# A decoder layer on one core: sums of gathered expert rows one step after their fetch, splits ordered behind them, residual work pinned to steps 32 to 46

## The chip, the core and the metric

The kernel runs on one core of a Trainium2 chip. The core has five engines that each work through a queue of their own in order: TensorE (PE, with its weight loads PEld), VectorE (DVE), ScalarE (ACT), GpSimd (POOL) and SyncE (SP, which here only issues transfers). Transfers run on 16 DMA engines. The metric is the device time of one execution in microseconds (us).

## The reference

One post-norm decoder layer on 256 tokens with 2048 channels. The part that the change touches is the last one, the sum over the chosen experts' output rows:

```python
u_sel = u[expert]
v_sel = v[expert]
act = jax.nn.gelu(jnp.einsum('td,thkd->thk', xc, u_sel).astype(jnp.float32), approximate=False)
return jnp.einsum('thk,thkd->td', (gate * act).astype(x.dtype), v_sel)
```

There are 16,384 experts, and every token takes 128 of them (8 heads of 16). Then `h = layer_norm(alpha * h + ffn)`.

## The kernel before

The kernel does not gather whole rows. For the first 1536 output channels it builds a dense matrix `S` of weights (expert by token, most of it zero) in SBUF and multiplies it on PE with the whole table `v_d`. For the last 512 channels it gathers the chosen rows of `v_g` by indirect DMA, one slot of 128 tokens at a time: 2 token tiles by 128 slots are 256 gathers of 256 KB, each followed by one multiply-add into `accg` on DVE (L813).

**The v stage.** It is the last long stage of the kernel. Its loop (L836) runs 124 steps `i2`. A step needs the weights of 128 experts (`weights`, L765: the part `step_of(i2)` of `S`, split in two) and three units of `v_d`, 128 x 512 each. I number the units through: unit m is unit m % 3 of step m // 3. Every float32 operand is split in a rounded part and a rest (`split`, L93): ACT casts `hi` (L94), DVE subtracts `lo` (L95). PE then does three products for each of the two token tiles (L119, L120, L121): six matmuls a unit, 18 a step. Four `hi`/`lo` pairs are in rotation, so splits run at most four units ahead of PE.

**Where the units lie.** A unit lands either in one of four `raw` buffers (`load_unit`, L100, on SP's queue) or in a part of `S` that is no longer needed (`v_unit`, L791). 23 units, all before step 13, use `raw`; all later ones use freed parts of `S`, which come free at the rate of half a part a step, so that loads run further and further ahead.

**Gathers.** `add_gathered` (L809) issues the gathers of a step on POOL (`v_gather`, L799) and writes each sum behind its gather. `spread` deals the 256 gathers out over steps 0 to 119. The rows land in three buffers `g`; from step `LEND` = 24 on, four of seven also use `raw`.

**Residual.** `residual` (L819) prepares alpha's operand for the last norm: 8 calls, written at even steps 32 to 46. Each loads two pieces of the first norm's scale and shift into the one buffer `g1` and two pieces of `z_dram` into `pre` (SP), and does four elementwise operations on POOL (L827, L828).

**The tail.** The last four steps are multiplied from `S` unsplit (L885), with weights copied into `last` (L854).

**What sets the order.** The program is written by a scheduler that sorts by priority and by its own estimate of times; `high_priority` draws the unit loads and splits ahead. `tc.issue_after(x)` adds one constraint: what is written in the block on the engine of x comes behind x in that engine's queue. What carries no such constraint may go far from where it is written.

Of the kernel before, what the change touches and what calls it, by code (L numbers as in the profile page):

```python
# [15 lines left out]
ALU = mybir.AluOpType  # L16
AX = mybir.AxisListType

P = 128
T = 256  # L20
NT = T // P
# [36 lines left out]
LEAD = 5  # L58
LAG = 1
KEEP0 = 40  # L60
LEND = 24
GL = 4
GVE = 120
ED = 2
EA = 2
TAIL_POOL = ((0, 1, 2), (0,))
# [5 lines left out]
def layer(ctx, tc, A, out):  # L72
    nc = tc.nc
# [14 lines left out]
        return psB.tile([P, 512], F32, name=name, tag="b")  # L88

    last_split, last_copy, last_load, last_moment = [None], [None], [None], [None]  # L90
    after_unit = [None]

    def split(hi, lo, src, eng=None):  # L93
        last_copy[0] = nc.scalar.copy(hi, src).ins  # L94
# [28 lines left out]
    e_idx = small.tile([P, NT, SLOTS], I32, name="e_idx")  # L123
# [3 lines left out]
    z_dram = dram.tile([NT, P, D], F32, name="z_dram")  # L127
# [368 lines left out]
    def step_of(i2, sl=slice(0, T)):  # L496
        return S[:, i2 // 2, sl.start // 2:sl.stop // 2, i2 % 2, :]
# [7 lines left out]
    def paired(a):  # L505
        return a.rearrange("p (t j) -> p t j", j=2)
# [156 lines left out]
    def spread(i, i0, i1):  # L663
        n = i1 - i0
        return gorder[len(gorder) * min(max(i - i0, 0), n) // n:len(gorder) * min(max(i - i0 + 1, 0), n) // n]
# [133 lines left out]
    def v_gather(i2, tt, slot):  # L799
        if i2 >= LEND and count[0] % (GB + RB) >= GB:  # L800
            g = raw_unit()
        else:
            g = gath.tile([P, GV], F32, name="g", bufs=GB)
        count[0] += 1
        nc.gpsimd.indirect_dma_start(out=g, out_offset=None, in_=A["v_g"],  # L805
                                     in_offset=bass.IndirectOffsetOnAxis(ap=e_idx[:, tt, slot:slot + 1], axis=0))
        return g

    def add_gathered(i2):  # L809
        with tc.issue_after(last_split[0]):  # L810
            for tt, slot in spread(i2, 0, GVE):
                g = v_gather(i2, tt, slot)
                nc.vector.scalar_tensor_tensor(accg[:, tt], g, pd[:, tt, slot:slot + 1], accg[:, tt],  # L813
                                               op0=ALU.mult, op1=ALU.add)


    pre = [[big.tile([P, 512], F32, name="pre", tag=f"{s}{q}") for q in (0, 3, 4, 5)] for s in "hl"]
# [1 line left out]
    def residual(c, hf):  # L819
        g1 = small.tile([P, 2, T], F32, name="g1", tag="h_gath")  # L820
        sl = slice(c * 512 + hf * T, c * 512 + (hf + 1) * T)
        for i in range(2):
            nc.sync.dma_start(g1[:, i], A["ln1"][i:i + 1, sl].broadcast_to([P, T]))
        for tt in range(NT):
            o = pre[tt][c][:, hf * T:(hf + 1) * T]
            nc.sync.dma_start(o, z_dram[tt][:, sl])
            nc.gpsimd.tensor_tensor(o, o, g1[:, 0], op=ALU.mult)  # L827
            nc.gpsimd.tensor_tensor(o, o, g1[:, 1], op=ALU.add)  # L828

    def finish(tt, c, lo, hi, src):  # L830
        o = pre[tt][c][:, lo:hi]
# [4 lines left out]
    for i2 in range(P - GL):  # L836
        wt = weights(i2, tokens if i2 == 0 else [slice(0, T)])
        units = []
        for c in range(NC):
            raw = v_unit(i2, c)  # L840
            units.append(load_unit(A["v_d"][i2 * NC + c], raw))
            if i2:
                for tt in range(NT):
                    product(wt, tt, c, units[c], i2)
        if i2 == 0:
            for tt in range(NT):
                for c in range(NC):
                    product(wt, tt, c, units[c], 0)
        add_gathered(i2)
        if 32 <= i2 < 48 and i2 % 2 == 0:  # L850
            residual((i2 - 32) // 4, (i2 - 32) // 2 % 2)
    last = [big.tile([P, 2, T], F32, name="last", tag="l2"), small.tile([P, 2, T], F32, name="last", tag="h_gath")]
    for j in range(GL):
        nc.scalar.copy(paired(last[j // 2][:, j % 2]), step_of(P - GL + j))  # L854
    for tt in range(NT):
        finish(tt, 3, 512 - GV, 512, accg[:, tt])
        nc.vector.bn_stats(stats[tt][:, 3], pre[tt][3])
# [96 lines left out]
```

## Time and profile before

| | us |
|---|---|
| median of 3 runs (lowest, highest) | 1741.95 (1739.28, 1742.34) |
| the profiled execution | 1739.89 |
| its span on the core | 1738.1 |
| PE busy | 1657.5 (95%) |
| DVE busy | 1434.8 (83%) |
| ACT busy | 899.2 (52%) |
| POOL busy | 884.1 (51%) |

The span runs from the first to the last instruction; 1.8 us of the execution lie around it. Busy shares are means over stages with different limits, so the stage that the change touches has to be read alone: by stretches of 20 us, by the timeline of each engine, and by what ended each idle time.

### The profile page before, as it was taken

What the parts mean: (1) busy time and instruction counts of PE and PEld (TensorE: products, weight loads), DVE (VectorE), ACT (ScalarE), POOL (GpSimd) and SP (SyncE); (2) the same over time, 40 slices, a digit from 0 to 9 for tenths busy, and PEclk for the clock granted to TensorE, in tenths of its full rate; (3) what the DMA queues carried; (4) which work ended last, traced back from release to release, by engine and by line L of the source; (5) the groups of instructions that cost most, each with busy time, mean ns of one, the idle gap of its engine ahead of it and who ended that gap; (6) DMA issues with size and microseconds to landing.
All of it is one profiled execution on the core that took longest, in us unless ns stands there. A gap on an engine that the chain in (4) does not pass through costs nothing. (4 is left out here: it accounts for less than half of the span.)

```text
span 1738.1 us, 33114 instructions
## 1 busy us (share of the span) xinstructions
PE 1657.5 (95%) x10652; PEld 1477.1 (85%) x10652; DVE 1434.8 (83%) x3483; ACT 899.2 (52%) x1917; POOL 884.1 (51%) x899
## 2 busy tenths in 40 slices
PE   8999999989899999999999889988999999999996
PEld 8999888879899999999999788876787888888883
DVE  6766677678999989888888798877888988889896
ACT  6545565444345555555554357774454555555551
POOL 0000000035886666566565588857657644556562
PEclk9999999989999999999999999999999999999998
DMA  6666767836688999999999942138899999999962
GB/s 219 177 188 191 197 187 248 261 99 198 212 281 299 336 359 327 329 343 348 346 327 336 300 131 61 51 104 280 300 328 344 386 341 330 338 311 331 353 197 89
DMA packets 206015, 451.13 MB, mean 260 GB/s; under 512 B 26929, under 2 KB 31473, under 8 KB 205329
## 3 DMA queue, kind: packets, MB, share of 16 engines
q1 hardware_dynamic: 164816, 297.93, 52.1%
q0 software_dynamic: 41024, 151.09, 25.2%
q8 instruction: 84, 1.38, 0.3%
q14 instruction: 91, 0.74, 0.1%
HBM read 444.59 MB, written 4.26 MB: 258 GB/s over the span
## 5 line engine op out<-in xcount | busy, mean ns | idle before, releaser
L94 ACT CAST hi<-S 128x512 fp32r<-128x512 f32 x677 | 420.0, 621 | 427.0 <-PE vacc L121 211.1
L95 DVE TENSOR_TENSOR lo<-S,hi 128x512 fp32r<-128x512 f32 x672 | 466.4, 705 | 84.9 <-ACT hi L94 78.7
L121 PE MATMUL ups<-hTh,lo 128*128 128x256 f32 x1408 | 390.9, 282 | 8.9 <-DVE lo L95 8.3
L119 PE MATMUL ups<-hTh,hi 128*128 128x256 f32 x1408 | 392.3, 280 | 4.0 <-ACT hi L94 4.0
L120 PE MATMUL ups<-hTl,hi 128*128 128x256 f32 x1408 | 392.2, 280 | 0.0
L659 POOL DMA_INDIRECT g<-u_g,e_idx x256 | 284.8, 1112 | 171.4 <-DVE g L684 124.2
L94 ACT CAST hi<-raw 128x512 fp32r<-128x512 f32 x327 | 201.8, 620 | 208.5 <-PE projT L120 57.5
L95 DVE TENSOR_TENSOR lo<-raw,hi 128x512 fp32r<-128x512 f32 x303 | 216.4, 719 | 110.4 <-ACT hi L94 108.4
L120 PE MATMUL vacc<-lo,wt 128*128 128x512 f32 x744 | 277.5, 399 | 6.8 <-DVE lo L95 6.7
L121 PEld LDWEIGHTS ups<-hTh,lo 128*128 128x128 f32 x1408 | 263.0, 188 | 13.5 <-DVE lo L95 12.2
L121 PE MATMUL vacc<-hi,wt 128*128 128x512 f32 x744 | 274.4, 396 | 0.0
L119 PEld LDWEIGHTS ups<-hTh,hi 128*128 128x128 f32 x1408 | 265.4, 189 | 5.0 <-ACT hi L94 5.0
L120 PEld LDWEIGHTS ups<-hTl,hi 128*128 128x128 f32 x1408 | 265.4, 189 | 0.0
L119 PE MATMUL vacc<-hi,wt 128*128 128x512 f32 x744 | 230.3, 397 | 7.7 <-ACT wt L94 6.7
L805 POOL DMA_INDIRECT g<-v_g,e_idx x139 | 161.3, 1161 | 127.0 <-DVE accg L813 107.2
L684 DVE SCALAR_TENSOR_TENSOR g<-g,h_gath 128x640 f32<-128x640 f32 x256 | 204.9, 820 | 16.7 <-DMA g<-u_g,e_idx 16.5
L805 POOL DMA_INDIRECT raw<-v_g,e_idx x117 | 138.2, 1181 | 84.2 <-DVE accg L813 64.4
L120 PEld LDWEIGHTS vacc<-lo,wt 128*128 128x128 f32 x744 | 139.7, 188 | 46.2 <-DVE lo L95 12.3
L119 PEld LDWEIGHTS vacc<-hi,wt 128*128 128x128 f32 x744 | 140.0, 189 | 42.8 <-ACT wt L94 7.3
L121 PEld LDWEIGHTS vacc<-hi,wt 128*128 128x128 f32 x744 | 140.2, 188 | 33.2 <-issue 0.5
L714 POOL TENSOR_SCALAR bt<-cst,slotT 128x128 f32<-128x128 f32 x192 | 126.5, 676 | 23.6 <-POOL bt L714 16.5
L294 POOL TENSOR_TENSOR bias<-bias,score 128x128 f32<-128x128 f32 (+1 forms) x16 | 11.9, 761 | 233.2 <-DMA bias<-relb 117.3
(243 smaller groups left out, 3070.9 us busy)
## 6 DMA issues: line engine op xcount, KB each, us to landing
S<-v_d SPq DMA_DIRECT2D x361, 256.0 KB, 5.5
S<-u_d SPq DMA_DIRECT2D x328, 256.0 KB, 5.4
raw<-w_t SPq DMA_DIRECT2D x100, 256.0 KB, 2.9
raw<-w_n SPq DMA_DIRECT2D x64, 256.0 KB, 3.0
raw<-w_o SPq DMA_DIRECT2D x64, 256.0 KB, 3.5
raw<-w_q SPq DMA_DIRECT2D x48, 256.0 KB, 3.3
bc<-i_dram SPq DMA_DIRECT2D x32, 256.0 KB, 3.2
raw<-u_d SPq DMA_DIRECT2D x24, 256.0 KB, 4.8
```

The source lines that it names most:

```text
L94: last_copy[0] = nc.scalar.copy(hi, src).ins
L95: last_split[0] = (eng or nc.vector).tensor_tensor(lo, src, hi.bitcast(F32), op=ALU.subtract).ins
L119: mm(o, l[0], r[0], start=first, stop=False)
L120: mm(o, l[0], r[1], start=False, stop=False)
L121: return mm(o, l[1], r[0], start=False, stop=last).ins
L294: nc.gpsimd.tensor_tensor(bias[:, tt, :n], bias[:, tt, :n], sel[:, tt, :n], op=ALU.add)
L659: nc.gpsimd.indirect_dma_start(out=g, out_offset=None, in_=table, in_offset=bass.IndirectOffsetOnAxis(ap=e_idx[:, tt, slot:slot + 1], axis=0))
L684: nc.vector.scalar_tensor_tensor(g, g, 1.0, h_gath[:, tt], op0=ALU.mult, op1=ALU.mult, accum_out=pd[:, tt, slot:slot + 1])
L714: eng.tensor_scalar(bt[j][:, i], iota, i2T[:, t:t + 1], None, op0=ALU.is_equal)
L805: nc.gpsimd.indirect_dma_start(out=g, out_offset=None, in_=A["v_g"], in_offset=bass.IndirectOffsetOnAxis(ap=e_idx[:, tt, slot:slot + 1], a ...
```

## The change

Five edits, all in the v stage:

- `add_gathered` issues a step's gathers and then writes the sums of the gathers of the step before (the list `fetched`). The last sum of each step is kept in `added`.
- The splits of step i2 are ordered behind the last sum written in step i2 - 2.
- Gathers run over steps 6 to 113 (`GV0`, `GVE`) in place of 0 to 119, and may use `raw` buffers from step 8 (`LEND`) in place of 24.
- The loads of `residual` are ordered behind the unit load last written, and its POOL work behind the last gather.
- The copies into `last` are ordered behind the last cast on ACT.

```diff
-LEND = 24
+LEND = 8
 GL = 4
-GVE = 120
+GV0 = 6
+GVE = 114
...
+    fetched, added = [], []
+
     def add_gathered(i2):
+
         with tc.issue_after(last_split[0]):
-            for tt, slot in spread(i2, 0, GVE):
-                g = v_gather(i2, tt, slot)
-                nc.vector.scalar_tensor_tensor(accg[:, tt], g, pd[:, tt, slot:slot + 1], accg[:, tt],
-                                               op0=ALU.mult, op1=ALU.add)
+            due = fetched[:]
+            fetched[:] = [(tt, slot, v_gather(i2, tt, slot)) for tt, slot in spread(i2, GV0, GVE)]
+            for tt, slot, g in due:
+                last_sum = nc.vector.scalar_tensor_tensor(accg[:, tt], g, pd[:, tt, slot:slot + 1], accg[:, tt],
+                                                          op0=ALU.mult, op1=ALU.add).ins
+        added.append(last_sum if due else None)
...
-        for i in range(2):
-            nc.sync.dma_start(g1[:, i], A["ln1"][i:i + 1, sl].broadcast_to([P, T]))
-        for tt in range(NT):
+        with tc.issue_after(last_load[0]), tc.issue_after(last_gather[0]):
+            for i in range(2):
+                nc.sync.dma_start(g1[:, i], A["ln1"][i:i + 1, sl].broadcast_to([P, T]))
+            for tt in range(NT):
...
-            units.append(load_unit(A["v_d"][i2 * NC + c], raw))
+
+            with tc.issue_after(added[i2 - 2]) if i2 >= 2 and added[i2 - 2] else nullcontext():
+                units.append(load_unit(A["v_d"][i2 * NC + c], raw))
...
-    for j in range(GL):
-        nc.scalar.copy(paired(last[j // 2][:, j % 2]), step_of(P - GL + j))
+    with tc.issue_after(last_copy[0]):
+        for j in range(GL):
+            nc.scalar.copy(paired(last[j // 2][:, j % 2]), step_of(P - GL + j))
```

The queues of all engines are the same up to the v stage. In it they differ in three places that matter below.

SP's queue at the head of the v stage, before (`pre<-z_dram` and `g...<-ln` are the loads of `residual`):

```order
L104 DMA raw<-v_d 128x512 x2
L823 DMA g_17206<-ln 128x256 x2
L104 DMA raw<-v_d 128x512 x2
L826 DMA pre<-z_dram 128x256 x14
L796 DMA S<-v_d 128x512
L826 DMA pre<-z_dram 128x256 x2
L823 DMA g_17300<-ln 128x256 x2
L104 DMA raw<-v_d 128x512 x5
```

and after:

```order
L105 DMA raw<-v_d 128x512 x4
L797 DMA S<-v_d 128x512
L105 DMA raw<-v_d 128x512 x5
L797 DMA S<-v_d 128x512 x2
L105 DMA raw<-v_d 128x512 x4
L797 DMA S<-v_d 128x512 x3
```

The scheduler had drawn all 16 loads of `z_dram` and the first scale and shift loads ahead by 32 steps; now the first of them stands behind the load of unit 113.

DVE's queue around the split of unit 31 (`raw_16233` before, `raw_16195` after), before:

```order
L95 TENSOR_TENSOR lo_16202<-S_4941,hi_16201 128x512
L813 SCALAR_TENSOR_TENSOR accg_15758<-g_16125,pd_6616,accg_15758 128x512
L95 TENSOR_TENSOR lo_16224<-raw_16221,hi_16223 128x512
L95 TENSOR_TENSOR wt_16217<-S_4941,wt_16217 128x256
L813 SCALAR_TENSOR_TENSOR accg_15758<-g_16128,pd_6616,accg_15758 128x512
L95 TENSOR_TENSOR lo_16236<-raw_16233,hi_16235 128x512
```

and after:

```order
L819 SCALAR_TENSOR_TENSOR accg_15758<-raw_16127,pd_6616,accg_15758 128x512
L819 SCALAR_TENSOR_TENSOR accg_15758<-raw_16129,pd_6616,accg_15758 128x512
L96 TENSOR_TENSOR lo_16186<-raw_16183,hi_16185 128x512
L819 SCALAR_TENSOR_TENSOR accg_15758<-raw_16131,pd_6616,accg_15758 128x512
L96 TENSOR_TENSOR wt_16179<-S_4941,wt_16179 128x256
L96 TENSOR_TENSOR wt_16223<-S_4941,wt_16223 128x256
L96 TENSOR_TENSOR lo_16198<-raw_16195,hi_16197 128x512
```

Gathered rows now take turns with units in the `raw` buffers: the buffer of unit 31 held the row of the first of these sums, with five rows between that sum and the unit's split; before, it held unit 23, whose split stood eight splits ahead. The same holds for unit 37, the last one in `raw`: its buffer comes free with a sum that only three rows part from its split.

POOL's queue at the first calls of `residual`, before (the sums of these gathers stand at steps 6 to 10, that of the `raw` one at step 31):

```order
L805 DMA g<-v_g,e_idx 128x512
L828 TENSOR_TENSOR pre<-pre,g_17394 128x256 x2
L805 DMA g<-v_g,e_idx 128x512 x3
L827 TENSOR_TENSOR pre<-pre,g_17491 128x256 x2
L828 TENSOR_TENSOR pre<-pre,g_17491 128x256 x2
L805 DMA g<-v_g,e_idx 128x512 x3
L805 DMA raw<-v_g,e_idx 128x512
```

and after (their sums stand at steps 43 to 46):

```order
L835 TENSOR_TENSOR pre<-pre,g_17280 128x256 x2
L806 DMA raw<-v_g,e_idx 128x512
L836 TENSOR_TENSOR pre<-pre,g_17280 128x256 x2
L806 DMA raw<-v_g,e_idx 128x512 x3
L806 DMA g<-v_g,e_idx 128x512 x3
L835 TENSOR_TENSOR pre<-pre,g_17377 128x256 x2
L806 DMA raw<-v_g,e_idx 128x512 x2
```

The four operations of a call now come once in seven gathers, between the gathers summed at steps 39 to 62.

## Rows read from the trace of the kernel before

**Rows 1.** Page, costliest groups: count | busy, mean ns | idle before, releaser.
```profile
L120 PE MATMUL vacc<-lo,wt 128*128 128x512 f32 x744 | 277.5, 399 | 6.8 <-DVE lo L95 6.7
...
L805 POOL DMA_INDIRECT g<-v_g,e_idx x139 | 161.3, 1161 | 127.0 <-DVE accg L813 107.2
```

**Rows 2.** Stretches of 20 us: busy (count) by engine, PEclk, DMA share, GB/s.
```profile
1180.00:1200.00 20.00, 19.11 (x74) 14.77 (x75) 16.34 (x23) 9.74 (x18) 15.31 (x15) 0.93 0.91 276
...
1340.00:1360.00 20.00, 20.00 (x86) 15.91 (x86) 18.55 (x32) 10.35 (x19) 16.21 (x13) 1.00 1.03 375
```

**Rows 3.** The same for tile `vacc` alone: PE, PEld, DVE.
```profile
1140.00:1160.00 20.00, 3.61 (x9) 1.46 (x9) 0.00 (x0) 1.00 0.19 44
```

**Rows 4.** PE's timeline: start, busy, what, [idle before <-releaser].
```profile
1163.75 0.50 PE L119 MATMUL vacc<-hi,wt 128*128 128x512 f32 x1 [0.89 <-ACT wt L94]
...
1180.02 1.22 PE L119 MATMUL vacc<-hi,wt 128*128 128x512 f32 x2 [5.76 <-ACT wt L94]
...
1234.36 0.50 PE L120 MATMUL vacc<-lo,wt 128*128 128x512 f32 x1 [1.98 <-DVE lo L95]
...
1326.67 0.49 PE L120 MATMUL vacc<-lo,wt 128*128 128x512 f32 x1 [1.06 <-DVE lo L95]
...
1422.54 0.63 PE L119 MATMUL vacc<-hi,wt 128*128 128x512 f32 x2
...
1423.94 0.63 PE L119 MATMUL vacc<-hi,wt 128*128 128x512 f32 x2
...
1699.27 3.59 PE L885 MATMUL vacc<-S,last 128*128 128x512 f32 x8
```

**Rows 5.** Waits of PE from 1162 to 1700 us: total, times, longest.
```profile
PE vacc L120 <- DVE lo L95: 6.7, 8, 2.0
```

**Rows 6.** SP's timeline at the head of the stage.
```profile
1158.38 7.09 SPq L826 DMA_DIRECT2D pre<-z_dram  x14
...
1172.16 0.81 SPq L823 DMA_DIRECT2D g<-ln  x2
1173.07 7.65 SPq L104 DMA_DIRECT2D raw<-v_d  x5
```

**Rows 7.** DVE's timeline: last copies before the stage, beside POOL's residual work, undisturbed.
```profile
1160.94 0.75 DVE L813 SCALAR_TENSOR_TENSOR accg<-g,pd,accg 128x512 f32<-128x512 f32 x1 [0.23 <-ACT pd L758]
...
1220.39 1.22 DVE L813 SCALAR_TENSOR_TENSOR accg<-g,pd,accg 128x512 f32<-128x512 f32 x1 [1.30 <-DMA g<-v_g,e_idx]
1221.54 1.23 DVE L95 TENSOR_TENSOR lo<-S,hi 128x512 fp32r<-128x512 f32 x1
...
1420.59 0.69 DVE L95 TENSOR_TENSOR lo<-S,hi 128x512 fp32r<-128x512 f32 x1 [0.64 <-ACT hi L94]
1421.20 0.74 DVE L813 SCALAR_TENSOR_TENSOR accg<-raw,pd,accg 128x512 f32<-128x512 f32 x1
1421.86 0.41 DVE L95 TENSOR_TENSOR wt<-S,wt 128x256 fp32r<-128x256 f32 x1
1422.20 0.74 DVE L813 SCALAR_TENSOR_TENSOR accg<-g,pd,accg 128x512 f32<-128x512 f32 x1
```

**Rows 8.** POOL's timeline: residual work among gathers, and a long gather.
```profile
1213.69 1.20 POOL L805 DMA_INDIRECT g<-v_g,e_idx  x1 [0.83 <-DVE accg L813]
...
1220.25 1.96 POOL L827 TENSOR_TENSOR pre<-pre,g 128x256 f32<-128x256 f32 x2
1222.18 2.32 POOL L828 TENSOR_TENSOR pre<-pre,g 128x256 f32<-128x256 f32 x2
...
1354.41 3.16 POOL L805 DMA_INDIRECT g<-v_g,e_idx  x1 [0.30 <-issue]
```

**Rows 9.** Issues from 1163 to 1245 us: count, KB each, median us to landing.
```profile
raw<-v_d SPq DMA_DIRECT2D x15, 256.0 KB, 5.7
...
g<-v_g,e_idx POOLq DMA_INDIRECT x23, 6.7
```

**Rows 10.** The same, whole span.
```profile
raw<-w_t SPq DMA_DIRECT2D x100, 256.0 KB, 2.9
```

More of the change, by code (lines that the diff above doesn't have):

```diff
@@ L90, in layer @@
     last_split, last_copy, last_load, last_moment = [None], [None], [None], [None]
-    after_unit = [None]
+    after_unit, last_gather = [None], [None]
     def split(hi, lo, src, eng=None):
@@ L804, in v_gather @@
         count[0] += 1
-        nc.gpsimd.indirect_dma_start(out=g, out_offset=None, in_=A["v_g"],
-                                     in_offset=bass.IndirectOffsetOnAxis(ap=e_idx[:, tt, slot:slot + 1], axis=0))
+        last_gather[0] = nc.gpsimd.indirect_dma_start(
+            out=g, out_offset=None, in_=A["v_g"],
+            in_offset=bass.IndirectOffsetOnAxis(ap=e_idx[:, tt, slot:slot + 1], axis=0)).ins
         return g
+    fetched, added = [], []
     def add_gathered(i2):
         with tc.issue_after(last_split[0]):
-            for tt, slot in spread(i2, 0, GVE):
-                g = v_gather(i2, tt, slot)
-                nc.vector.scalar_tensor_tensor(accg[:, tt], g, pd[:, tt, slot:slot + 1], accg[:, tt],
-                                               op0=ALU.mult, op1=ALU.add)
+            due = fetched[:]
[4 more added lines that the diff above has]
+        added.append(last_sum if due else None)
     pre = [[big.tile([P, 512], F32, name="pre", tag=f"{s}{q}") for q in (0, 3, 4, 5)] for s in "hl"]
@@ L821, in residual @@
         sl = slice(c * 512 + hf * T, c * 512 + (hf + 1) * T)
-        for i in range(2):
-            nc.sync.dma_start(g1[:, i], A["ln1"][i:i + 1, sl].broadcast_to([P, T]))
-        for tt in range(NT):
[L825 to L828, printed above, removed]
+        with tc.issue_after(last_load[0]), tc.issue_after(last_gather[0]):
+            for i in range(2):
+                nc.sync.dma_start(g1[:, i], A["ln1"][i:i + 1, sl].broadcast_to([P, T]))
+            for tt in range(NT):
+                o = pre[tt][c][:, hf * T:(hf + 1) * T]
+                nc.sync.dma_start(o, z_dram[tt][:, sl])
+                nc.gpsimd.tensor_tensor(o, o, g1[:, 0], op=ALU.mult)
+                nc.gpsimd.tensor_tensor(o, o, g1[:, 1], op=ALU.add)
     def finish(tt, c, lo, hi, src):
@@ L849, in layer @@
         add_gathered(i2)
+        if i2 == P - GL - 1:
+            add_gathered(P)
         if 32 <= i2 < 48 and i2 % 2 == 0:
```

## The prediction

> **What bounds the kernel now.** All engines' queues are unchanged up to the v stage, so I read that stage alone. First PE's timeline in a stretch without trouble: a unit of six matmuls starts at 1422.54 us and the next at 1423.94, so a unit takes 1.40 us, a matmul 0.233, a step 4.20 [rows 4]. In the stretch 1340 to 1360 us PE is busy for all 20 us, while DVE has 18.55 and POOL 16.21 [rows 2]: PE sets the pace there. Then the ends of the stage. It begins at 1163.75 and the tail's matmuls begin at 1699.27 [rows 4], 535.5 us. The stage has 3 x 744 = 2232 matmuls [rows 1]; nine ran ahead of it [rows 3] and eight stand behind the tail's first by PE's order, which leaves 2215, or 516.8 us. **So 18.7 us are lost**, and all of it lies before 1326.67, the last row on which PE stood idle: from there to 1699.27 are 372.6 us, 1597 matmuls at full pace [rows 4].
>
> The loss has three parts. One gap of 5.76 us ends at 1180.02 [rows 4]. Its cause is on SP: 14 loads of `z_dram` take its queue from 1158.38 for 7.09 us, and the unit loads behind them begin at 1173.07 only, after a scale and shift load that waited for POOL to give back `g1` [rows 6]. Behind this gap the granted clock of the stretch is 0.93 [rows 2]: some matmuls ran at the lower of PE's two levels, 1.2 in place of 2.4 GHz. The remaining gaps are mostly waits for a DVE split, 6.7 us in eight listed waits, 1.98 the longest [rows 5, 4]; DVE had been held by a sum whose row had not landed, as at 1220.39 (1.30 us) [rows 7]. A listed gap undercounts, since the matmul before it is drawn as ending late; I use the 18.7 us.
>
> **The change part by part.** *Start of the stage.* Two sums leave DVE's queue ahead of its last copies; the one at 1160.94 held the next instruction for 0.67 us, and PE stood for 0.89 us before 1163.75 [rows 7, 4]. I take 0.7 us off, bounds 0 and 0.9.
>
> *The residual loads leave SP's head.* The gap of 5.76 us and the slow clock behind it go. What is late next: unit 9 needs the buffer of unit 4, split some 4 us into the stage by the four-pair rotation; with 5.7 us to landing [rows 9] and 1.3 us of cast and split it is ready near 11 us, and PE, which has nine units of 1.40 us less the nine matmuls done early to do first, wants it at 10.5 to 12.1. So at most half a microsecond stays.
>
> *Sums one step later, seven buffers from step 8.* Before, up to step 32 a sum stood 3 to 7 splits behind the sum that freed its buffer (mostly 5 or 6 by the order, 7.0 to 8.4 us at PE's pace), and a gather takes 6.7 us to land [rows 9], plus about 0.3 for the hand-over and its place in POOL's queue. That margin is what DVE kept running out of. After, the distance is 9 splits, 12.6 us, for 192 of 253 gathers, and 6 for eight. Margin 5 us: DVE should not wait in an undisturbed step. DVE's own work has room: 3 x 0.61 + 0.34 + 2.37 x 0.66 = 3.73 us a step of 4.20 (start to start in [rows 7]; 256 sums over 108 steps). So the 18.7 us go, and the following come back.
>
> *Units 31 and 37.* Their `raw` buffers come free with a sum (the second place of the order). From that sum a load has 0.3 us to issue, 5.7 to land [rows 9], 0.6 for the cast: 6.6 us. DVE's rows between take 2 x 0.66 + 0.61 + 2 x 0.34 = 2.6 us for unit 31 and 0.61 + 2 x 0.34 = 1.3 us for unit 37, so DVE is held 4.0 and 5.3 us. It is ahead of PE by at most four units less cast and split, 5.6 - 1.3 = 4.3 us, but one gather just before has only seven rows between its buffer's release and its sum (about 4.2 us against 7.0), which eats 2.8 of that. PE then waits 4.0 - 1.5 = 2.5 us at unit 31, and at unit 37, with the lead regained only by 0.5 us a step, 5.3 - 1.5 = 3.8. Sum 6.3. From below: if the loads land in 2.9 us, as on a quiet queue [rows 10], both lose 2.8, and about 1 us is left; from above, with both leads gone, 9.3. I take **6**, since five unit loads and three gathers stand in front of each.
>
> *Residual work in steps 38 to 62.* 32 POOL operations now lie beside dense sums. On POOL seven gathers cost 7 x 1.31 us (1213.69 to 1220.25 is five), and the four operations 4.25 (1220.25 to 1224.50) [rows 8]: 13.4 us against the 12.4 that seven gathers have. POOL slips by 1.0 us a call, 8 us in all. On DVE a sum or split beside them takes 1.22 or 1.23 in place of 0.74 or 0.69 [rows 7]; 0.5 us for each operation is 0.67 us a step, so DVE needs 4.40 a step and slips by 0.2, 5 us in all. The cover is the gathers' margin of 5 us and DVE's lead of 4.3. I take a loss of **1.5** us, bounds 0 and 8.
>
> The Trainium skill (SBUF — State Buffer, "Who interferes with whom") says that a VectorE instruction with two SBUF inputs and a GpSimd one that reads SBUF contend, and that the second to issue fully blocks. Sums, splits and these POOL operations are all of that kind. The trace shows half: DVE loses about 0.5 us beside an operation of about 1 us. By the rule DVE would lose the whole operation; this is in rival 2.
>
> *DMA.* A step moves 3.5 units (half a one for running ahead) and 2.37 gathers of 0.262 MB in 4.20 us, 366 GB/s, plus 4.2 MB of residual loads in steps 33 to 62, 34 GB/s. 375 GB/s ran with PE full [rows 2]; units run 14 or more ahead there, so nothing is taken off.
>
> *`last` copies.* Four ACT copies move behind the last cast; they end some 3 us before the tail. Nothing.
>
> *Small restarts* like those that hide in the 18.7 us: 1 us, bounds 0 and 2.
>
> Sum: - 18.7 - 0.7 + 6 + 1.5 + 1 = - 10.9 us, from the profiled 1739.9 to 1729.0. The median of the runs lies 2.1 above the profiled execution, so **1731** for a median.
>
> **Rivals.** (1) *Loads land fast.* SP's queue behind units 31 and 37 is held, so little is in flight. With 2.9 us to landing [rows 10] only 1 of the 6 us is lost: 1726. Against it: 5.7 us is what the same transfers took [rows 9].
>
> (2) *Steps 38 to 62 are bound by DVE or POOL.* If DVE loses a whole operation of 1.0 us each time, that is 32 us over 24 steps, 1.33 a step: it needs 5.06, slips 0.86 a step, 21 us, less 4.3 of lead: 16. If POOL slips 2 us a call (one long gather in each), 16 less 9 of cover: 7. Between these, a loss of about 9 in place of 1.5: 1738.5.
>
> (3) *POOL sets the pace: slower than before.* A gather of 3.16 us stands in the trace [rows 8]. Seven buffers leave POOL 12.4 us for seven gathers and a call; if a gather costs s, the eight calls lose 8 x (7 s + 4.25 - 12.4) less 9.3 us of cover. The whole gain of 19.4, with 7 already lost, is used up when this is 12: s = 1.55. At s = 1.8 it is 26 us: 1755. For it: the mean gather is 1.16 busy [rows 1] and 0.3 apart, 1.46, close below. Against it: back to back the trace has 1.31.
>
> (4) *The change doesn't take away the waits.* If DVE was held by unit loads rather than by sums, the small gaps stay: 18.7 less the 5.76 gap and the slow clock behind it (about 1.4) is 11.5, of which most stays; the gain is 8, of which 6 go to units 31 and 37: 2 us, 1740.
>
> **How the numbers follow.** The forecast, 1731 (1727 to 1735 by its bounds), gets 0.58; rival 1 0.13; rival 2 0.17; rival 3 0.05; rival 4 0.07. A measurement can tell some 0.2%, 3.5 us, from no change. Faster is the forecast, rival 1 and half of rival 2 (1738.5 is on that edge): 0.80. Slower is rival 3: 0.05. The same is the rest of rival 2 and rival 4: 0.15. The range from 1724.5 to 1739 holds the forecast, rival 1 and half of rival 2 (0.58 + 0.13 + 0.085, 0.8), and leaves out rivals 3 and 4 and the upper end of rival 2.
>
> **What would show it.** Right: no gap over 1 us in PE's timeline before step 8; two gaps of 2 to 4 us about 40 and 52 us into the stage, each with ACT waiting for a `raw` unit; no wait of DVE for gathered rows outside steps 8 to 13 and 38 to 62; POOL without idle time in steps 38 to 62. Wrong: gaps all through steps 38 to 62 (rivals 2 and 3), split waits before step 8 (rival 4), or no gap at units 31 and 37 (rival 1).

## The result: slower by 1%, and the profile after

The changed kernel took 1758.51 us in the median of 5 runs (1756.57 to 1767.75), the kernel before 1741.95. The ratio is 1.0098, its 95% interval 1.0080 to 1.0116. The forecast was 1731, with 1739 as its upper end: wrong in size and in sign.

The profiled execution took 1759.56 us with a span of 1757.8, 19.7 more than before. I divide it where the prediction did:

| profiled execution, us | before | after |
|---|---|---|
| first matmul of the dense v stage | 1163.75 | 1168.35 |
| from there to the tail's first matmul | 535.5 | 551.5 |
| of that lost, after 0.2333 us for each matmul | 18.7 | 33.7 |
| from the tail's first matmul to the end | 38.8 | 37.9 |

The stage starts 4.6 us later, loses 15.0 more, and has four more matmuls in it (0.9 us) that were behind the tail's first before; the tail is 0.9 shorter by them. Together that is the 19.7, but for rounding.

**The later start** comes from code that is the same in both. PE's stretches of 40 us near 1000 us (busy, count, granted clock, DMA share, GB/s), before:

```profile
960.00:1000.00 40.00, 32.12 (x234) 0.96 0.93 308
1000.00:1040.00 40.00, 34.59 (x281) 1.00 0.44 136
```

and after:

```profile
960.00:1000.00 40.00, 30.46 (x209) 0.90 0.86 282
1000.00:1040.00 40.00, 35.94 (x278) 0.93 0.52 155
```

0.06 and 0.07 of 40 us are 5.2 us at full pace that the lower granted clock took. The queues are the same there. In the runs below, whose queues are all the same up to the stage, it started between 1163.1 and 1167.2 on one chip, between 1169.4 and 1173.0 on another; the changed kernel itself started at 1164.56 in its profile of group 4. It goes with the execution, not with the change, so I leave it out of what follows. The last stretch ahead of the stage did get shorter. PE's last transposes in front of it, first before, then after:

```profile
1160.33 0.38 PE L757 MATMUL wTp<-cst,slotT 128*128 128x128 f32 x2
1165.60 0.38 PE L758 MATMUL wTp<-cst,slotT 128*128 128x128 f32 x2
```

From there to the first matmul of the stage are 3.42 us before and 2.75 after, so the two sums that left DVE's queue are worth the 0.7 us of the forecast, and what came ahead of them cost 5.3.

**The stage.** What DVE waited for in it (total us, times, longest), before:

```profile
DVE accg L813 <- DMA g<-v_g,e_idx: 23.9, 22, 3.2
DVE accg L813 <- DMA raw<-v_g,e_idx: 2.8, 2, 1.4
...
DVE wt L95 <- ACT wt L94: 0.4, 1, 0.4
```

and after:

```profile
DVE wt L96 <- ACT wt L95: 34.1, 41, 2.4
DVE accg L819 <- DMA g<-v_g,e_idx: 1.9, 2, 1.4
```

The waits for gathered rows went from 26.7 us to 1.9, as the change and the forecast had it. A wait that was next to nothing before took their place: the weight split on DVE (`wt`) now waits for the weight cast on ACT, 41 times. And PE, which had waited 6.7 us for splits [rows 5], waits almost three times as long:

```profile
PE vacc L121 <- DVE lo L96: 18.8, 15, 2.3
PE vacc L120 <- ACT hi L95: 4.8, 2, 3.9
```

PE's timeline has the places (start, busy, what, idle before and its releaser):

```profile
1213.85 1.99 PE L120 MATMUL vacc<-hi,wt 128*128 128x512 f32 x4 [3.94 <-ACT hi L95]
1224.92 1.26 PE L120 MATMUL vacc<-hi,wt 128*128 128x512 f32 x4 [0.86 <-ACT hi L95]
...
1335.82 0.50 PE L121 MATMUL vacc<-lo,wt 128*128 128x512 f32 x1 [1.37 <-DVE lo L96]
...
1365.36 0.50 PE L121 MATMUL vacc<-lo,wt 128*128 128x512 f32 x1 [2.31 <-DVE lo L96]
1375.86 0.50 PE L121 MATMUL vacc<-lo,wt 128*128 128x512 f32 x1 [1.82 <-DVE lo L96]
...
1454.40 0.50 PE L121 MATMUL vacc<-lo,wt 128*128 128x512 f32 x1 [1.82 <-DVE lo L96]
...
1502.69 0.50 PE L121 MATMUL vacc<-lo,wt 128*128 128x512 f32 x1 [1.82 <-DVE lo L96]
...
1653.32 0.50 PE L121 MATMUL vacc<-lo,wt 128*128 128x512 f32 x1 [1.82 <-DVE lo L96]
```

Four gaps of exactly 1.82 us, two of them (1502.69 and 1653.32) far behind the last residual work, where neither a gather nor a unit is late. Something fixed in the queues makes them. Here is DVE before the one at 1502.69:

```profile
1494.22 1.89 DVE L96 TENSOR_TENSOR lo<-S,hi 128x512 fp32r<-128x512 f32 x3
1496.75 0.42 DVE L96 TENSOR_TENSOR wt<-S,wt 128x256 fp32r<-128x256 f32 x1 [0.64 <-ACT wt L95]
1497.09 1.41 DVE L819 SCALAR_TENSOR_TENSOR accg<-raw,pd,accg 128x512 f32<-128x512 f32 x2
1500.95 0.43 DVE L96 TENSOR_TENSOR wt<-S,wt 128x256 fp32r<-128x256 f32 x1 [2.45 <-ACT wt L95]
1501.29 0.74 DVE L819 SCALAR_TENSOR_TENSOR accg<-raw,pd,accg 128x512 f32<-128x512 f32 x1
1501.95 1.89 DVE L96 TENSOR_TENSOR lo<-S,hi 128x512 fp32r<-128x512 f32 x3
```

and ACT beside it:

```profile
1497.68 0.62 ACT L95 CAST hi<-S 128x512 fp32r<-128x512 f32 x1 [0.96 <-ACT wt L95]
1499.04 0.62 ACT L95 CAST hi<-S 128x512 fp32r<-128x512 f32 x1 [0.73 <-PE vacc L122]
1499.97 0.62 ACT L95 CAST hi<-S 128x512 fp32r<-128x512 f32 x1 [0.31 <-PE vacc L122]
1500.49 0.42 ACT L95 CAST wt<-S 128x256 fp32r<-128x256 f32 x1
```

DVE's queue at this place holds the splits of units 216, 217 and 218, the weight split of step 73, two sums, **the weight split of step 74**, one more sum, and only then the splits of units 219, 220 and 221, which belong to step 73. The weights of step 74 are split ahead of all three units of the step before it. On ACT the cast that this split needs stands behind the cast for unit 222, which needs the pair of unit 218 back from PE. So DVE waits until PE has used up unit 218, with the splits of 219 to 221 behind it in the queue: the lead of DVE over PE, up to four units, falls to nothing. From the weight cast on, PE is behind a weight split (0.34 us start to start), a sum (0.66) and a split.

In the order of the kernel before, 123 weight splits stand right behind the first unit split of their own step; after, 68 stand just ahead of it, two (steps 11 and 13) by two units more, and seven (steps 39, 45, 47, 55, 63, 74 and 109) by a whole step. The order that the change adds holds the unit splits behind sums; the weight splits, written ahead of them, carry no such order, so the scheduler moves them forward.

To see what each place costs I took, from PE's timeline, the start of each unit's first matmul against that of the unit before, less 1.40 us. Before, the sum of these delays over the stage is led by 6.85 us at the gap of [rows 4], the rest at early units. After (a row takes only units that are over 0.3 us late; what is smaller stands in the last row):

| where | lost, us |
|---|---|
| units 31 to 33 and 37 | 6.8 (5.8 and 1.0) |
| the seven early weight splits (units 114, 132, 138, 162, 186, 219, 324) | 13.9 |
| slow clock behind the last two of these | 3.1 |
| other places between units 113 and 190, where the residual work lies | 7.9 |
| all else | 2.0 |

The first line is the loads of units 31 and 37. The chain of work that ended last goes through both (start, us from issue to landing, what):

```profile
1206.21 6.94 DMA raw<-v_d
1220.26 3.91 DMA raw<-v_d
```

Of the 5.8 us some 1.8 are slow clock: the granted clock was 0.91 from 1200 to 1220 us.

The slow clock of the third line is seen in the stretches (PE busy, count, granted clock, DMA share, GB/s):

```profile
1480.00:1500.00 20.00, 20.00 (x87) 1.00 1.02 371
1500.00:1520.00 20.00, 18.18 (x72) 0.91 0.91 314
1640.00:1660.00 20.00, 18.18 (x72) 0.91 0.92 329
```

72 matmuls in place of 87 are 3.5 us lost in a stretch; 1.82 is the gap itself, the rest was spent at the lower level of 1.2 GHz, to which the granted clock fell after PE had stood.

**The fourth line.** POOL at the second call of the residual (same columns as the timelines above):

```profile
1342.33 1.44 POOL L835 TENSOR_TENSOR pre<-pre,g 128x256 f32<-128x256 f32 x2
1343.93 1.26 POOL L806 DMA_INDIRECT raw<-v_g,e_idx  x1 [0.16 <-issue]
1345.20 1.45 POOL L836 TENSOR_TENSOR pre<-pre,g 128x256 f32<-128x256 f32 x2
```

and DVE:

```profile
1342.07 5.14 DVE L96 TENSOR_TENSOR lo<-S,hi 128x512 fp32r<-128x512 f32 x3
```

Three splits take 1.88 us elsewhere (1349.46 in the same stretch, 1494.22 above: 1.89). Here they take 5.14, 3.26 more, beside two pairs of POOL operations of 1.44 and 1.45. Over the stage DVE's operations beside POOL's residual work run 20.6 us over their usual time, 2.6 a call. A call of the residual comes once in seven gathers, about three steps, and DVE gains no more than 0.5 us a step on PE.

### The profile page after: what moved, and what is told of

Its sections match the earlier page's. It is cut to its first block, busy times and chain, and to the rows that moved or that the text cites. A ratio compares the mean times of both kernels' runs of the same rounds, so it can differ in the third digit from the quotient of the medians.

```text
span 1757.8 us, 33187 instructions
## 1 busy us (share of the span) xinstructions
PE 1667.1 (95%) x10652; PEld 1482.9 (84%) x10652; DVE 1439.6 (82%) x3483; ACT 899.6 (51%) x1917; POOL 895.7 (51%) x899
## 5 line engine op out<-in xcount | busy, mean ns | idle before, releaser
L121 PE MATMUL vacc<-lo,wt 128*128 128x512 f32 x744 | 291.7, 402 | 18.8 <-DVE lo L96 18.8
L122 PE MATMUL vacc<-hi,wt 128*128 128x512 f32 x744 | 288.4, 398 | 0.0
L806 POOL DMA_INDIRECT raw<-v_g,e_idx x144 | 169.2, 1175 | 123.7 <-DVE accg L819 46.1
L120 PE MATMUL vacc<-hi,wt 128*128 128x512 f32 x744 | 221.4, 398 | 5.7 <-ACT hi L95 4.8
L806 POOL DMA_INDIRECT g<-v_g,e_idx x112 | 142.8, 1275 | 60.4 <-DVE accg L819 37.8
```

The lines of the kernel that those rows point to most:

```text
L120: mm(o, l[0], r[0], start=first, stop=False)
L121: mm(o, l[0], r[1], start=False, stop=False)
L122: return mm(o, l[1], r[0], start=False, stop=last).ins
L806: last_gather[0] = nc.gpsimd.indirect_dma_start(out=g, out_offset=None, in_=A["v_g"], in_offset=bass.IndirectOffsetOnAxis(ap=e_idx[:, tt, ...
```

## Experiments

The runs were made on several chips, and a run is compared only with the kernel before, or with another run, on its own chip: before took 1741.2 us in the first group's medians, 1758.5 in the second's, 1752.8 in the third's and 1742.0 in the last's. "Lost" is the loss in the stage of the run's profiled execution, counted as in the first table. It is that of one execution, not of the median: the changed kernel lost 33.7, 36.7 and 35.4 us in its three profiles.

### Group 1: one part undone, one part alone

Theory A is the early weight splits, theory B the residual work.

**Weight splits held** (`lead_split` keeps the split of a step's first unit):

```diff
+    lead_split = [None]
 ...
         for sl in tts:
+          with tc.issue_after(lead_split[0]) if i2 >= 2 else nullcontext():
             split(paired(wt[0][:, sl]), paired(wt[1][:, sl]), step_of(i2, sl))
 ...
                 units.append(load_unit(A["v_d"][i2 * NC + c], raw))
+            if c == 0:
+                lead_split[0] = last_split[0]
```

> The changed kernel, with one order added: a step's weight split on DVE stands behind the split of the first unit of the step before. In the changed kernel seven weight splits (steps 39, 45, 47, 55, 63, 74 and 109) stand ahead of all three unit splits of the step before; DVE waits there for ACT's cast of the weights, which waits for PE. Theory A (these seven early weight splits are the loss): 13.9 us of delays at units 114, 132, 138, 162, 186, 219 and 324 and 3.1 us of slow clock behind the last two go, 1758.5 to about 1741.5, and no PE gap near steps 73 and 108. Theory B (the residual work of POOL slows DVE, and the seven are only where a loss shows that would come anyway): the five inside steps 38 to 62 come back at other units, only the two outside go: about 1752. Theory C (the loss is at units 31 and 37, for want of raw buffers): 1758.

Measured 1746.18, ratio 1.0027 (1.0014 to 1.0040), against 1.0098: 0.7% or some 12 us gained, between the two theories. Its profile, the slowest of ten runs (1750.42), lost 26.3 us. In it the stretches that held the two late gaps are whole (busy, count, clock, DMA share, GB/s):

```profile
1500.00:1520.00 20.00, 20.00 (x87) 1.00 1.04 387
1640.00:1660.00 20.00, 20.00 (x87) 1.00 1.01 367
```

so outside the residual's steps A holds to the letter. Inside them 14.5 us are still lost (17.8 before the edit: the 7.9 of the table and five of the seven places). I take it that DVE has so little in hand there that taking one hold-up away lets the next one show; no run shows that alone.

**The order between sums and splits taken out:**

```diff
-            with tc.issue_after(added[i2 - 2]) if i2 >= 2 and added[i2 - 2] else nullcontext():
-                units.append(load_unit(A["v_d"][i2 * NC + c], raw))
+            units.append(load_unit(A["v_d"][i2 * NC + c], raw))
```

> The changed kernel without the order that puts the splits of a step behind the sums of two steps before; sums still come a step after their fetch. By DVE's order every weight split from step 14 on then stands behind the first unit split of its own step, as before the change, and 28 sums stand behind the last split (8 before the change). Theory A (early weight splits): the same 17 us go, 1758.5 to about 1741.5, less or more by what the 28 late sums do to the tail (28 x 0.66 = 18.5 us of DVE, beside 22 us of the tail's matmuls: 0 to 8 us). Theory B (POOL's residual work): about 1752 with gaps in steps 38 to 62 still there.

Measured 1757.45, ratio 1.0093 (1.0060 to 1.0127): no gain. Yet the stage lost only 8.1 us, and no weight split stands a whole step early any more. What is left is mostly units 31 to 33 and 37 (7.5 us). The residual work, which lies at 1320.9 to 1471.7 us here, costs PE nothing that shows (PE busy, count, granted clock, DMA share, GB/s):

```profile
1340.00:1360.00 20.00, 20.00 (x88) 1.00 1.02 362
1360.00:1380.00 20.00, 20.00 (x87) 1.00 0.99 344
```

PE has no listed wait from 1240 to 1690 us, though DVE's operations beside the residual work run 18.9 us over their usual time, almost as in the changed kernel. So it is the added order that hands these hold-ups on to PE: with it the splits wait for the sums, without it the sums fall behind.

The time came back in the tail, 63.4 us from its first matmul in place of 37.9. DVE's sums (count, ns least/median/most, first and last start), first of the changed kernel, then of this run:

```profile
L819 DVE SCALAR_TENSOR_TENSOR accg<-raw,pd,accg x144: 733/744/1672, 1205.0 to 1686.3; 128x512 f32<-128x512 f32 x144
```

```profile
L819 DVE SCALAR_TENSOR_TENSOR accg<-raw,pd,accg x144: 733/746/1262, 1204.8 to 1730.5; 128x512 f32<-128x512 f32 x144
```

The last sum is 44 us later. In the tail POOL is at its limit, one gather behind the other:

```profile
1702.50 1.06 POOL L806 DMA_INDIRECT g<-v_g,e_idx  x1 [0.30 <-issue]
1703.87 1.26 POOL L806 DMA_INDIRECT g<-v_g,e_idx  x1 [0.30 <-issue]
```

28 sums that slide behind the last split cost not 18.5 us of DVE, as I had it in the expectation, but 28 gathers of about 1.4 us on POOL, 39 us, which made the tail 25.5 us longer than in the changed kernel. So the added order has a use: it keeps the sums, and with them the gathers, on time.

**Residual work of POOL left out** (28 of 32 operations):

```diff
-                nc.gpsimd.tensor_tensor(o, o, g1[:, 0], op=ALU.mult)
-                nc.gpsimd.tensor_tensor(o, o, g1[:, 1], op=ALU.add)
+                if (c, hf) == (3, 1):
+                    nc.gpsimd.tensor_tensor(o, o, g1[:, 0], op=ALU.mult)
+                    nc.gpsimd.tensor_tensor(o, o, g1[:, 1], op=ALU.add)
```

> The changed kernel with 28 of the 32 residual operations of POOL left out (alpha's operand keeps the first norm's scale and shift only in its last piece); all loads stay. Seven weight splits still stand early in DVE's order (steps 39, 43, 45, 47, 55, 74, 109). Theory A: the seven gaps of 1.5 to 2.5 us stay, and only the other losses of steps 38 to 62, 7.9 us, go: 1758.5 to about 1750.5. Theory B: all losses of steps 38 to 62 go, 17.8 us, and the two later ones stay: about 1740.5.

Measured 1749.06, ratio 1.0037 (1.0018 to 1.0057): 9.4 us below the changed kernel's median, near A's 7.9 and far from B's 18. In steps 38 to 47 PE's gaps now stand at the early weight splits and nowhere else (PE's timeline, gaps only):

```profile
1330.41 0.50 PE L121 MATMUL vacc<-lo,wt 128*128 128x512 f32 x1 [1.36 <-DVE lo L96]
...
1349.30 0.50 PE L121 MATMUL vacc<-lo,wt 128*128 128x512 f32 x1 [1.82 <-DVE lo L96]
...
1370.28 0.50 PE L121 MATMUL vacc<-lo,wt 128*128 128x512 f32 x1 [1.82 <-DVE lo L96]
```

Both causes are real with the order in place, and they overlap in these steps.

**The kernel before with the residual pinned, alone:**

```diff
-        for i in range(2):
+        with tc.issue_after(last_load[0]), tc.issue_after(last_gather[0]):
+            for i in range(2):
```

> The kernel before, with one part of the change alone: the residual loads ordered behind the unit load last written, and POOL's residual work behind the last gather. What the forecast says: the gap ending at 1180.02, the slow clock behind it and part of the small gaps beside POOL's work go, some 9 to 11 us, and 1 to 3 come back in steps 32 to 60: 1742 to about 1734. Theory B (POOL's residual work among the sums is dear wherever it stands): 9 go and 8 or more come back: about 1741. If the first units simply wait for something else: 1742.

Measured 1743.68, ratio 1.0019 (1.0005 to 1.0033). The stage lost 4.4 us in place of 18.7, and the tail took it back: 52.7 us in place of 38.8. By DVE's order 18 sums stand behind the last split (8 before), the last of them starts at 1712.3, and DVE waits for gathers among them. So the 5.76 us gap and its followers were worth some 14 us in the stage, more than the 9 to 11 of the expectation, and are not worth it in the kernel as long as nothing keeps the gathers on time.

### Group 2: residual late, raw buffers later

All but the last start from the changed kernel.

**Weight splits held, and raw buffers for gathers from step 13:**

```diff
-LEND = 8
+LEND = 13
```

> The run with the weight splits held (1746.2), and gathers may use raw buffers from step 13 in place of 8. By DVE's order units 30, 31 and 37 then have 11, 8 and 13 units between their buffer's release and their split (5, 1 and 1 before). If the loss at units 31 to 37 (8.8 us there) is for want of raw buffers: it goes, and 1 to 3 us come back since the first gathers have three buffers only: about 1739. If these loads are late for another reason (the transfers are slow at that time): 1746.

Measured 1759.03, ratio 1.0010 (0.9988 to 1.0032), no more than a hint of a gain over 1.0027 on another chip. In the profile units 31 and 37 come on time; 0.67 us is the largest delay before unit 46. (The weight splits of steps 11 and 13, which stood just ahead of these two units, are no longer early in this run either; that PE waited for the loads is read from the chain above.) The first gathers have three buffers only, and DVE waits 10.7 us for their rows up to 1300 us. Elsewhere it lost more, 29.2 us in all.

**The same with the residual calls written at steps 114 to 117:**

```diff
-        if 32 <= i2 < 48 and i2 % 2 == 0:
-            residual((i2 - 32) // 4, (i2 - 32) // 2 % 2)
+        if GVE <= i2 < GVE + 4:
+            residual(i2 - GVE, 0)
+            residual(i2 - GVE, 1)
```

> As the run before in this list, and the eight residual calls written at steps 114 to 117, so that POOL's residual work lies behind the last gather (34 us from about step 113 on, where DVE has no sums). If POOL's residual work among the sums is what still costs in steps 41 to 68 (14.5 us with the weight splits held): 1739 less 14.5, about 1725, and 3 to 5 us lost in the stage in all. If DVE is short of time there by the dense sums alone: about 1737, gaps in steps 40 to 70 still there. If the residual work now holds up the tail: 1730 or more, with PE waiting before its last 48 matmuls.

Measured 1759.15, ratio 1.0003 (0.9984 to 1.0021). The stage's loss is halved, 14.5 us, and steps 41 to 56 have no gap over 0.6 us; the residual's crowd was the cause there. But the tail took 54.8 us. DVE in the tail:

```profile
1726.63 1.79 DVE L842 SCALAR_TENSOR_TENSOR pre<-pre,accg 128x512 f32<-128x512 f32 x2 [21.48 <-POOL pre L838]
```

The eight calls share one `g1`, so each waits for the one before it and then for its load; on POOL:

```profile
1711.82 1.41 POOL L837 TENSOR_TENSOR pre<-pre,g 128x256 f32<-128x256 f32 x2 [3.97 <-DMA g<-ln]
```

I had counted 34 us of POOL's work and no waits between the calls; it took 54 us, from 1673 to 1727.

**The same without holding the weight splits:**

> As the run before in this list, without holding the weight splits. By DVE's order six of them (steps 47, 55, 63, 74, 109 and 117) stand ahead of all three unit splits of the step before. If such a place costs some 2 us by itself, without any residual work beside it, and some slow clock behind some of them: 12 to 17 us more than the run before, 1737 to 1742. If it costs only where DVE has no lead anyway: the same as the run before, about 1726.

Measured 1768.49, ratio 1.0053 (1.0029 to 1.0077): 9.3 us over the run before, a little under the 12 to 17 expected. The stage lost 24.2 us, 9.7 more than in the run before, and the tail took 49.6 in place of 54.8, so part of it hides behind the late residual. All six places show, five of them before any residual work (here the last, which has some beside it):

```profile
1685.64 0.50 PE L121 MATMUL vacc<-lo,wt 128*128 128x512 f32 x1 [1.82 <-DVE lo L96]
```

**The kernel before with the residual pinned and late:**

```diff
-        if 32 <= i2 < 48 and i2 % 2 == 0:
-            residual((i2 - 32) // 4, (i2 - 32) // 2 % 2)
+        if 112 <= i2 < 120:
+            residual((i2 - 112) // 2, i2 % 2)
```

> The kernel before with the residual pinned (as in the run of before with that alone), but written at steps 112 to 119. By DVE's order 5 sums stand behind the last split, 18 with the calls at steps 32 to 46. If what took back the 14 us won in the stage there was the sums that had fallen behind (POOL's residual work holds the gathers, and the order lets the last sums slide into the tail): the stage loses 5 to 6 us and the tail is as before, 1741 less 14: about 1727. If the tail is long for another reason, the residual's own results for one: 1741.

Measured 1779.14, ratio 1.0119 (1.0094 to 1.0144). It fell on both counts: 21.9 us lost in the stage, and a tail of 69.3. It shares the late residual with the second run of this group, so it doesn't tell what late sums alone would do; that rests on the two runs of group 1.

### Group 3: the changed kernel again, and the residual spread out

**The changed kernel:**

> The changed kernel itself, beside the next three on their chip. 1.0098 of before on the first chip; 1.010 is expected here, with delays of about 2 us at units 114, 132, 138, 162, 186, 219 and 324. The clock near 1000 us, in code that the change does not touch, is slow for longer in some executions than in others: nothing is made of it here.

Measured 1763.70, ratio 1.0057 (1.0036 to 1.0078). Its profile has delays at the same units, 1.5 to 3.3 us at each of the seven and 7.5 us at units 31 to 33.

**Weight splits held, `LEND = 13`, one residual call in twelve steps:**

```diff
-        if 32 <= i2 < 48 and i2 % 2 == 0:
-            residual((i2 - 32) // 4, (i2 - 32) // 2 % 2)
+        if 16 <= i2 < 112 and i2 % 12 == 4:
+            residual((i2 - 16) // 24, (i2 - 16) // 12 % 2)
```

> The changed kernel with the weight splits held, raw buffers for gathers from step 13, and the eight residual calls spread out: written at steps 16, 28, ... 100 in place of 32, 34, ... 46, so that four POOL operations come once in 28 gathers, not once in 7. If the loss with the weight splits held (27.0 us in the stage) was units 31 to 37 (8.8) and the crowding of sums, splits and residual work (14.5): the first goes, of the second some 2 us are left, and nothing waits in the tail; 1.0027 less 21/1742, about 0.991 of before. If dense sums alone keep DVE without a lead: 1.000.

Measured 1751.80, ratio 0.9990 (0.9969 to 1.0010): 0.7% below the changed kernel beside it, and level with before, not 0.9% below it. The profiled execution lost 29.2 us, 16.7 of it at units 38, 148 and 334 and right behind them.

**The same with `LEND = 8`:**

> The same with raw buffers for gathers from step 8 as in the changed kernel: the loss at units 31 to 37 comes back and nothing else, 7 to 9 us more than the run before in this list, about 0.996 of before. If the raw buffers are no cause: the same as the run before.

Measured 1756.17, ratio 1.0016 (0.9997 to 1.0035). 4.4 us over the run before, with intervals that overlap. In the profile 7.3 us are lost at units 31 to 33 and 37, as in the changed kernel, but the stop at unit 38 (4.0 us in the run before) is gone, and DVE waits 4.9 us for gathered rows in place of 17.5. So raw buffers from step 13 take one loss away and bring part of it back as late rows. This profile, the fastest of ten runs, lost 19.8 us in all, less than that of the run before, whose median is lower: profiles of single executions don't rank these two.

**The kernel before with the order between sums and splits, alone** (sums still in the step of their gathers):

```diff
+        last_sum = None
         with tc.issue_after(last_split[0]):
 ...
-                nc.vector.scalar_tensor_tensor(accg[:, tt], g, pd[:, tt, slot:slot + 1], accg[:, tt],
-                                               op0=ALU.mult, op1=ALU.add)
+                last_sum = nc.vector.scalar_tensor_tensor(accg[:, tt], g, pd[:, tt, slot:slot + 1], accg[:, tt],
+                                               op0=ALU.mult, op1=ALU.add).ins
+        added.append(last_sum)
 ...
-            units.append(load_unit(A["v_d"][i2 * NC + c], raw))
+            with tc.issue_after(added[i2 - 2]) if i2 >= 2 and added[i2 - 2] else nullcontext():
+                units.append(load_unit(A["v_d"][i2 * NC + c], raw))
```

> The kernel before with one part of the change alone: the splits of a step ordered behind the last sum of two steps before. By DVE's order three weight splits (steps 10, 13 and 116) then stand ahead of all three unit splits of the step before. If such a place costs about 2 us and sometimes slow clock: 5 to 9 us more than before, 1.004. If the order is harmless where sums aren't dense: 1.000. If it is a gain by itself, since sums no longer slide to the end: below 0.998.

Measured 1768.54, ratio 1.0090 (1.0058 to 1.0121), above the dearest case of the expectation. The third early place shows with the same 1.82 us:

```profile
1692.07 0.50 PE L120 MATMUL vacc<-lo,wt 128*128 128x512 f32 x1 [1.82 <-DVE lo L95]
```

But most of its 38.5 us are lost before step 29, where splits now stand behind sums that wait for gathers (31.7 us of such waits on DVE). Without the sums put a step later this order hands every wait for a gather on to PE.

### Group 4: is it lumps or late units?

The order as it stands gathers DVE's queue into lumps, two or three sums and then three splits. A finer one (the split of unit c behind the c-th sum of two steps before, for which `added` keeps all sums of a step; the weight split behind the last unit split of the step before):

```diff
-            with tc.issue_after(added[i2 - 2]) if i2 >= 2 and added[i2 - 2] else nullcontext():
-                units.append(load_unit(A["v_d"][i2 * NC + c], raw))
+            held = added[i2 - 2] if i2 >= 2 else []
+            with tc.issue_after(held[min(c, len(held) - 1)]) if held else nullcontext():
+                units.append(load_unit(A["v_d"][i2 * NC + c], raw))
```

> As the spread-out run (weight splits held, raw buffers from step 13, residual calls at steps 16 to 100), but the order between sums and splits is made fine: the split of a step's first unit stands behind the first sum of two steps before, that of the second behind the second, of the third behind the last; and the weight split behind the last unit split of the step before. By DVE's order sums and splits then take turns (13 places with two sums in a row and none with three, against 61 and 13; 14 places with three splits in a row, against 83). If these lumps, three sums and then three splits, are what still takes DVE's lead: under 10 us lost in the stage, and some 0.7% less than the spread-out run beside it. If units that land late are what is left: no difference between the two.

Beside it the spread-out run again:

> The spread-out run again, beside the run with the fine order, on its chip: 0.999 of before there as on the last chip; 30 us lost in the stage of that profile, half of it at three units. If these three stops came by chance: others, at other units.

and the changed kernel:

> The changed kernel itself, beside the two, on their chip: 1.006 to 1.010 of before. With the spread-out run 0.7 to 1.1% below it, if the three things found (early weight splits, crowded residual work, raw buffers shared too early) are the loss.

Measured, in this order: 1735.99, ratio 0.9964 (0.9953 to 0.9975); 1735.45, ratio 0.9965 (0.9947 to 0.9982); 1757.38, ratio 1.0089 (1.0070 to 1.0108). The fine order makes no difference (14.0 and 13.9 us lost), so the lumps cost nothing that can be seen here. On this chip the three repairs bring 21.9 us, from 1757.38 to 1735.45, about as much as the stages of the two profiles differ (35.4 and 13.9 us lost), and the result is 0.35% below the kernel before.

The spread-out run shows why spacing matters. POOL and DVE beside one of its calls:

```profile
1403.87 2.42 POOL L837 TENSOR_TENSOR pre<-pre,g 128x256 f32<-128x256 f32 x2
1406.26 1.18 POOL L838 TENSOR_TENSOR pre<-pre,g 128x256 f32<-128x256 f32 x1
```

```profile
1403.32 1.23 DVE L821 SCALAR_TENSOR_TENSOR accg<-raw,pd,accg 128x512 f32<-128x512 f32 x1
1404.47 1.23 DVE L821 SCALAR_TENSOR_TENSOR accg<-g,pd,accg 128x512 f32<-128x512 f32 x1
1405.62 2.97 DVE L96 TENSOR_TENSOR lo<-S,hi 128x512 fp32r<-128x512 f32 x3
```

Summed over the stage, the sums and splits of DVE that are drawn longer run 20.6 us over their usual 0.745, 0.69 and 0.415 us in the changed kernel, and 23.0 us here. The hold-ups are as large as in the changed kernel; a call only comes every twelve steps, so DVE has time to regain its lead by the next, and PE loses about 1 us a call (gaps of 0.98 and 1.27 at two of them) in place of the crowd's.

## Why the prediction was wrong, step by step

The sum gave 1729.0 for a profiled execution; it took 1759.56, 30.6 more. By its terms:

| term | forecast | found | difference |
|---|---|---|---|
| old loss goes | - 18.7 | - 18.7 | 0 |
| two sums less ahead of the stage | - 0.7 | - 0.7 | 0 |
| slow clock near 1000 us | none | + 5.3 | 5.3 |
| units 31 and 37 | 6 | 6.8 | 0.8 |
| residual work in steps 38 to 62 | 1.5 | 7.9 | 6.4 |
| small restarts | 1 | 2.0 | 1.0 |
| early weight splits and slow clock | none | 17.0 | 17.0 |

- **The step that failed: the order between splits and sums stood in the sum at nothing.** The prediction spoke of it only as what sets the distance of sums, and never asked what it does to the rest of DVE's queue. The run without it (group 1), in which 28 sums slid into the tail, lost 8.1 us in the stage, against the 8.5 that the sum had left there (6, 1.5 and 1): what the stage of the changed kernel lost beyond the forecast came by the order. It did so in two ways. It leaves the weight splits free, and the order of the changed kernel showed seven of them a step early before any run; these places made 13.9 us, and slow clock behind two of them 3.1. Held back, the two late ones vanished whole; those among the residual work gave back only part (group 1). And it makes splits wait for sums, so that what slows the sums reaches PE; that is the next term.
- **The residual term was mis-sized**: 7.9 us in place of 1.5, at the upper bound of 8 that I had set, and in the steps that I had named. I took 0.5 us for each POOL operation, 16 us of DVE beside 34 of POOL, from rows in which POOL itself was slowed (pairs of operations in 1.96 and 2.32 us [rows 8]) and DVE half as much [rows 7]. In the changed kernel DVE lost 20.6 us beside 27.2 of POOL, 0.64 for each operation. At 1342 us a pair ran in 1.44 us and DVE stood for all of it (3.26 us against 2.89). The rule of the Trainium skill (SBUF — State Buffer, "Who interferes with whom"), by which the second of the two to issue is fully blocked, agrees with this row better than the row I trusted. At the last two calls of the same run, from 1421 and 1435 us, POOL's pairs took 2.15 to 2.44 us, so there both were slowed. With 0.64 in the sum, DVE slips 9.2 us in place of 5 in the 24 steps. The gathers' margin, which I also set against this, covers late rows, and DVE waited only 1.9 us for rows; the lead of 4.3 alone leaves 4.9, an estimate by the prediction's own sum, and the rest of the 7.9 is not accounted for. Rival 2 had the mechanism and, for this term alone, about the size (9).
- **Units 31 and 37** came out near the sum, 6.8 us against 6, and that is partly luck: 5.8 and 1.0 us in place of 2.5 and 3.8. The two loads took 6.94 and 3.91 us to land, not 5.7 each, and the 5.8 hold 1.8 us of slow clock that was not in the sum. Rival 1 (fast landing) fell for unit 31 and came nearer the truth for unit 37. `LEND = 13` took both losses away.
- **The old loss went** (the table takes it all as gone; what may be left of it lies in the 2.0 of the small restarts): no gap over 1 us before step 10, and DVE's waits for gathers from 26.7 us to 1.9. Rival 4 fell. The pinned residual alone took 14 us off the stage of the kernel before.
- **Rival 3** (POOL at its limit) did not happen in the stage of the changed kernel. It is what happened in the tail of the run without the added order: gathers at 1.4 us, one behind the other.
- **The start.** The 0.7 us came as worked out, but all that stands ahead of the stage came 5.3 us late by the clock near 1000 us, in code that is the same; other runs on a common chip started up to 4.1 us apart. A chance of that size belongs in a range, and was not in it.

What stays open: the changed kernel with all three repairs still loses 13.9 us in its stage where the forecast left 8.5, and 29.2 on another chip. One stop stands in both profiles, at unit 38 (4.7 and 4.0 us), where ACT waits for a unit (2.55 and 2.46 us) and DVE for a gathered row (4.20 and 3.54); it is not there with raw buffers from step 8. The stops at units 148 and 334 of the second profile are not in the first, and the profile names nothing that they waited for. Why they come on one chip and not on the other was not tried.

## What to carry to other kernels

An ordering constraint moves what it does not name. After adding one, read the queue for the instructions that it leaves free, and ask of each that came forward what it waits for and who stands behind it. An order also ties what it names: whatever makes the first late now makes the second late. And a gain in a stage is a gain only if the work that was late there is not pushed into the tail: compare the last start of each side job before and after.

## What the runs showed of the hardware

- DVE operations on 128x512 beside POOL operations on 128x256 took from 1.2 to 3.7 us in place of 0.7, and who was slowed differed: POOL too in the kernel before and at 1421 us of the changed one, DVE alone at 1342 us there.
- The kernel before took 1741.2 to 1758.5 us in the median by chip, 1% apart, as much as was in question here. Ratios moved too: the changed kernel's were 1.0098, 1.0057 and 1.0089 in its three comparisons.
- A gap of 1.82 us in PE cost 3.5 where the clock fell behind it (two of the four shown), and 2.0 where it didn't.
